# Three waits tied by hand around the merge of two attention branches

## The chip, the core and the metric

The kernel runs on one NeuronCore of a Trainium2 chip, in float32. The metric is the device time of one execution in microseconds. Its engines are TensorE (PE in the profile, with PEld for its weight loads), VectorE (DVE), ScalarE (ACT), GpSimd (POOL) and SyncE (SP, which here only issues DMAs). Each works through its own instructions in order and waits for others by semaphores. DMAs are issued from the queues of SP, ACT or POOL: an issue that waits holds up all that stands behind it in that queue.

## The reference

One layer on 512 tokens plus 16 learned meta tokens, width 1024. The normalised input `xn` goes into two attention branches of 8 heads each, `o_sb` (stick-breaking) and `o_df` (differential, with a norm of its own for each head). Cut to what the change touches:

```python
o_df = (rmsnorm(o_df, subln_g[l]) * (1.0 - lam_init)).transpose(0, 2, 1, 3).reshape(B, L_pad, DF_V_W)
y_sb = o_sb @ w_br_sb[l]
y_df = o_df @ w_br_df[l]
gates = jax.nn.sigmoid(xn @ w_gate[l] + b_gate[l]).reshape(B, L_pad, 2, D)
merged = gates[:, :, 0] * y_sb + gates[:, :, 1] * y_df
h = h + merged @ w_out[l]
```

Then follow a SwiGLU feed-forward part with a residual and a last norm.

## The kernel before

**Products.** Every float32 operand is held as a high part (rounded to the matmul's format) and a low part, the rest. `split` (lines 77 to 79) makes them: ScalarE casts the high part (`wh`, L78), VectorE subtracts to get the low one (`wl`, L79). A product is three matmuls per 128 rows of the contraction: L290 (high by high), L291 (high weight by low activation) and L292 (low weight by high activation). PE can so start on a weight when `wh` is there, and stops at the first L292 when `wl` is not.

**Weights.** They come in chunks of 512 KB in a fixed list (`stream`), loaded by SP into three `wst` buffers and split two chunks ahead of use. A buffer is loaded again when its `wl` is done.

**The gates.** `gate` (L805) computes one block of 128 channels (f, of 8) of one branch's gate (br, 0 or 1) for all 512 tokens: 24 matmuls into one PSUM bank, of which there are four for this, then an evacuation by ScalarE with the bias (L807). The gates of f = 0 are computed early and stored in DRAM (`g_part`). Those of f = 1 and 2 (`sg0`, `sg1`) are computed during the last two heads; their evacuation adds the bias, and their sigmoids are taken in place at L1053. From f = 3 on the evacuation itself is a sigmoid.

**The last head's norm.** `norm` in `df_head` (L767 to L776) takes a Ln and an Exp on ScalarE (L771, L772), two products on VectorE (L773, L774), and makes the head's output `o_h` on ScalarE (L775) and `o_l` on VectorE (L776). The last head's norm is run between the matmuls of the gates of f = 2.

**The branch outputs.** `y_units` multiplies two heads at a time with a slice of the branch's weight (matmuls named `o_h`, `o_l`), evacuates each f on ScalarE (L796, into `y_out`) and stores it from GpSimd's queue into DRAM with an accumulating DMA (L800, `y_df<-y_out`).

**The merge** (from L1055). For f in the order 1, 2, 0, 3 to 7: SP loads the sums back (`y_sb`, `y_df`, L1065), two f ahead. They lie in memory that the attention used before, so the first of these loads wait for the attention's last reader. GpSimd multiplies gate and output in place (L1122; VectorE for f = 6 and 7), VectorE adds the two products (L1126, into `mf` for f below 4), and `merge_sums` (L1087) splits the sum and combines it with others for the output product, which is made of seven products of half size. Each branch has two gate tiles, so f = 0 uses the tiles of f = 1 again: the stored gates are loaded into them (L1117) once the sum of f = 1 is done, and only then comes their sigmoid (L1118). The residual `x` is loaded into `hres` from GpSimd's queue, four DMAs of 512 KB (L1133).

**What sets the order.** Past the start, a scheduler puts each engine's instructions in order by its own estimate of when they can run; the order is then fixed. `tc.add_manual_dep` tells it that one instruction comes behind another. Activation table loads are put in where a function is not in the set that is loaded.

## Time and profile before

| | |
|---|---|
| median of 3 runs | 950.56 us (948.53 to 2375.36) |
| profiled execution, its own time | 949.31 us |
| its span, first to last instruction | 947.5 us |
| instructions in the span | 16049 |
| mean granted clock of TensorE | 0.997 |
| DMA moved | 158.41 MB, mean 167 GB/s |

Of the three runs two lie within 2 us of the profiled one. In the profile's rows a line such as `L79` is a line of the kernel; times in a timeline are microseconds from the start of the span, first the start, then the duration; what stands in brackets is how long the engine sat idle before and what ended that. A row of waits gives the total in us, the number of times and the longest.

### The profile page before, as it was taken

The page shows a single profiled execution, that of the slowest core. Times are in us where ns is not written, and L with a number is a line of the kernel's source. Part 1 is how long each engine was busy: PE and PEld are TensorE (multiplying, and loading weights), DVE is VectorE, ACT ScalarE, POOL GpSimd, SP SyncE. Part 2 cuts the span into 40 slices and gives each one's busy share as a digit, 9 for nine tenths or more (in the row PEclk, how much of TensorE's full clock was granted, in tenths as well). Part 3 has the DMA queues.
Part 4 walks back from the last instruction along what each step waited for, and adds up shares of the span by engine and source line. Part 5 has one row for each costly group of instructions (what it writes and reads, how often), then busy time and mean ns, then how long its engine had stood idle before and what let it go on. Part 6 is the DMA issues. An engine that isn't in the chain of part 4 may idle for free.

```text
span 947.5 us, 16049 instructions
## 1 busy us (share of the span) xinstructions
PE 929.5 (98%) x6009; PEld 843.6 (89%) x6010; DVE 733.9 (77%) x1400; ACT 586.3 (62%) x1105; POOL 186.8 (20%) x211
## 2 busy tenths in 40 slices
PE   8999999999999999999999899999999999999997
PEld 5988999898999999999887688899999999978886
DVE  6988878776678766787653578899888888989875
ACT  6665676676656666666774355765555555566654
POOL 3000121222323344344504330001000000000013
PEclk9999999999999999999999999999999999999999
DMA  8525778778767889799958854537743343286642
GB/s 248 143 68 157 176 170 203 168 164 251 192 198 184 196 190 190 162 208 191 198 155 203 262 172 163 144 80 175 158 124 112 93 131 90 68 259 202 198 153 89
DMA packets 155823, 158.41 MB, mean 167 GB/s; under 512 B 6465, under 2 KB 117218, under 8 KB 155746
## 3 DMA queue, kind: packets, MB, share of 16 engines
q1 hardware_dynamic: 132690, 101.61, 35.9%
q0 software_dynamic: 22896, 55.72, 28.8%
q8 instruction: 47, 0.77, 0.3%
q14 instruction: 30, 0.25, 0.1%
q10 hardware_dynamic: 160, 0.07, 0.0%
HBM read 133.64 MB, written 50.86 MB: 195 GB/s over the span
## 4 chain that ended last, share of the span: by engine, by line
PE 76%; DVE 12%; issue 4%; ACT 3%; DMA 3%; POOL 1%; SPq 0%; POOLq 0%; ACTq 0%; DVEq 0%
PE mm L292 17%; PE mm L291 17%; PE mm L290 17%; PE z L290 6%; PE z L291 6%; PE z L292 6%; DVE wl L79 3%; DVE s L636 2%; PE z L705 1%; PE z L704 1%; ACT wh L78 1%; PE tr L555 1%; DMA wsu<-in_w_in_dram 1%; DVE s L637 1%; DVE s L632 1%
## 5 line engine op out<-in xcount | busy, mean ns | idle before, releaser
L292 PE MATMUL mm<-xT_h,wl 128*128 128x264 f32 (+2 forms) x656 | 213.5, 325 | 3.3 <-DVE wl L79 3.3
L291 PE MATMUL mm<-xT_l,wh 128*128 128x264 f32 (+2 forms) x656 | 214.3, 327 | 0.5
L290 PE MATMUL mm<-xT_h,wh 128*128 128x264 f32 (+2 forms) x656 | 214.3, 327 | 0.5 <-ACT xT_h L909 0.5
L79 DVE TENSOR_TENSOR wl<-wst,wh 128x1024 fp32r<-128x1024 f32 (+1 forms) x147 | 166.4, 1136 | 31.1 <-ACT wh L78 30.7
L78 ACT CAST wh<-wst 128x1024 fp32r<-128x1024 f32 (+1 forms) x147 | 141.8, 966 | 76.2 <-PE mm L291 55.2
L292 PEld LDWEIGHTS mm<-xT_h,wl 128*128 128x128 f32 x656 | 124.0, 189 | 13.7 <-DVE wl L79 3.7
L290 PEld LDWEIGHTS mm<-xT_h,wh 128*128 128x128 f32 x656 | 124.0, 189 | 10.4 <-ACT xT_h L909 0.9
L291 PEld LDWEIGHTS mm<-xT_l,wh 128*128 128x128 f32 x656 | 123.8, 189 | 10.4 <-DVE xT_l L910 1.3
L290 PE MATMUL mm<-hT_h,wh 128*128 128x256 f32 x304 | 85.9, 284 | 1.2 <-ACT qx L1317 0.8
L292 PE MATMUL mm<-hT_h,wl 128*128 128x256 f32 x304 | 85.9, 284 | 0.0
L291 PE MATMUL mm<-hT_l,wh 128*128 128x256 f32 x304 | 85.8, 283 | 0.0
L290 PEld LDWEIGHTS mm<-hT_h,wh 128*128 128x128 f32 x304 | 57.9, 191 | 1.8 <-ACT qx L1317 1.2
L292 PEld LDWEIGHTS mm<-hT_h,wl 128*128 128x128 f32 x304 | 58.1, 191 | 0.0
L291 PEld LDWEIGHTS mm<-hT_l,wh 128*128 128x128 f32 x304 | 58.1, 191 | 0.0
L708 DVE CUSTOM_DVE_ANT_0 pr<-z,bias 128x144 f32<-128x144 f32 (+3 forms) x64 | 30.9, 501 | 34.2 <-PE z L705 31.9
L290 PE MATMUL mm<-o_h,wh 128*128 128x512 f32 x128 | 53.2, 415 | 0.1
L291 PE MATMUL z<-wl,da 128*128 128x512 f32 (+1 forms) x132 | 50.4, 382 | 0.6 <-DVE wl L79 0.6
L291 PE MATMUL mm<-o_l,wh 128*128 128x512 f32 x128 | 50.1, 391 | 0.3 <-DVE o_l L776 0.3
L290 PE MATMUL z<-wh,da 128*128 128x512 f32 (+1 forms) x132 | 50.3, 381 | 0.0
L1432 POOL TENSOR_TENSOR outs<-hres,gF 128x512 f32<-128x512 f32 x4 | 6.2, 1548 | 223.6 <-DVE hres L1418 216.8
L292 PE MATMUL z<-wh,da 128*128 128x512 f32 (+1 forms) x132 | 50.2, 380 | 0.0
L292 PE MATMUL mm<-o_h,wl 128*128 128x512 f32 x128 | 50.2, 392 | 0.0
(366 smaller groups left out, 2515.5 us busy)
## 6 DMA issues: line engine op xcount, KB each, us to landing
wst<-in_w_in_dram SPq DMA_DIRECT2D x40, 512.0 KB, 5.9
ds<-in_w_ffn_down_dram POOLq DMA_DIRECT2D x30, 512.0 KB, 6.1
wst<-in_w_ffn_gate_dram SPq DMA_DIRECT2D x22, 512.0 KB, 4.0
wsu<-in_w_ffn_up_dram SPq DMA_DIRECT2D x20, 512.0 KB, 3.8
wst<-in_w_gate_dram SPq DMA_DIRECT2D x16, 512.0 KB, 8.6
y_df<-y_out POOLq DMA_DIRECT2D x32, 256.0 KB, 7.2
slots<-ds SPq DMA_DIRECT2D x13, 512.0 KB, 3.3
os<-in_w_out_dram POOLq DMA_DIRECT2D x12, 512.0 KB, 4.6
```

The costliest lines, as they stand in the source:

```text
L78: cast["last"] = (hi_copy or nc.scalar.copy)(hi, src)
L79: (lo_eng or nc.vector).tensor_tensor(lo, src, hi.bitcast(F32), op=ALU.subtract)
L290: nc.tensor.matmul(ps, lhsT=ah, rhs=bh, start=(start and i == 0), stop=False, skip_group_check=skip)
L291: nc.tensor.matmul(ps, lhsT=ah, rhs=bl, start=False, stop=False, skip_group_check=skip)
L292: nc.tensor.matmul(ps, lhsT=al, rhs=bh, start=False, stop=(stop and i == n - 1), skip_group_check=skip)
L555: nc.tensor.transpose(pt[:, (t - j) * P:(t - j + 1) * P], blocks(t, j * P, (j + 1) * P), ident)
L632: nc.vector.scalar_tensor_tensor(s, zz, 0.0, e, op0=ALU.max, op1=ALU.add)
L636: nc.vector.tensor_tensor_scan(f, resets[:, L - (b - a):][:, ::-1], f, BIG, op0=ALU.mult, op1=ALU.add)
L637: nc.vector.tensor_tensor(s, zz, s, op=ALU.subtract)
L704: nc.tensor.matmul(o, lhsT=q[c][:, qs], rhs=k[c][:, 0, k0:k1], start=True, stop=False)
L705: nc.tensor.matmul(o, lhsT=q[c][:, qs], rhs=k[c][:, 1, k0:k1], start=False, stop=True)
L708: nc.vector.tensor_tensor_reduce(po, zz, bb, scale=1.0, scalar=-3.0e38, op0=ALU.add, op1=ALU.max, accum_out=mx[:, t, c:c + 1])
```

## The change

Three ties are added with a new helper, `behind(ins, name)`, which makes an instruction wait for one that was remembered in `cast` under that name.

```diff
     def split(hi, lo, src, lo_eng=None, hi_copy=None):
         cast["last"] = (hi_copy or nc.scalar.copy)(hi, src)
-        (lo_eng or nc.vector).tensor_tensor(lo, src, hi.bitcast(F32), op=ALU.subtract)
+        cast["lo"] = (lo_eng or nc.vector).tensor_tensor(lo, src, hi.bitcast(F32), op=ALU.subtract)
+
+    def behind(ins, name):
+        tc.add_manual_dep(ins.ins, cast[name].ins.name,
+                          mybir.DependencyInfo(mybir.DependencyClass.Sync, mybir.DependencyReason.DATA))
...
         split(wh, wl, staged[n], nc.gpsimd if n < 3 else None)
+        cast["split"] = cast["lo"]
...
-            nc.scalar.activation(sq, sq, AF.Exp, scale=-0.5)
+            cast["norm"] = nc.scalar.activation(sq, sq, AF.Exp, scale=-0.5)
...
     for sg in sg0 + sg1:
-        nc.scalar.activation(sg, sg, AF.Sigmoid)
+        behind(nc.scalar.activation(sg, sg, AF.Sigmoid), "norm")
...
-            (nc.gpsimd if f < 6 else nc.vector).tensor_tensor(sg[br], sg[br], y, op=ALU.mult)
+            if f < 6:
+                cast["gated"] = nc.gpsimd.tensor_tensor(sg[br], sg[br], y, op=ALU.mult)
+            else:
+                nc.vector.tensor_tensor(sg[br], sg[br], y, op=ALU.mult)
...
-        nc.vector.tensor_tensor(m, sg[0], sg[1], op=ALU.add)
+        merged = nc.vector.tensor_tensor(m, sg[0], sg[1], op=ALU.add)
+        if 2 < f < KT - 1:
+            behind(merged, "split")
...
     for t in range(NQ):
-        nc.gpsimd.dma_start(hres[:, t], xv[:, t])
+        behind(nc.gpsimd.dma_start(hres[:, t], xv[:, t]), "gated")
```

The sum of two gated outputs (f = 3 to 6) comes behind the last weight's low part that the program has asked for, the loads of `hres` behind GpSimd's last product, and the four sigmoids of f = 1 and 2 behind the last norm's Exp. (The helper also replaces the two lines in `c2` that did the same by hand.) No operation is added to what the kernel computes. Lines behind the edits have larger numbers in the new kernel: L771 becomes L775, L775 L779, L800 L804, L1053 L1057, L1122 L1127, L1133 L1142. The scheduler, given the ties, moves a few instructions.

ScalarE's queue around the last head's norm, before. `sq` is the norm's variance, `sg_...` a gate tile, `wh` a weight's high part, `o_h` the head's output:

```order
L78 CAST sqh_5819<-sq_5818 128x512
L771 ACT_TABLE_LOAD
L771 ACTIVATE sq_5818<-tr_5846,eps_c_179 128x512
L807 ACTIVATE sg_5825<-mm_5827,pcol_165 128x512
L772 ACT_TABLE_LOAD
L772 ACTIVATE sq_5818<-sq_5818 128x512
L78 CAST wh_5944<-wst_5828 128x1024
L1053 ACT_TABLE_LOAD
L1053 ACTIVATE sg_5825<-sg_5825 128x512
L775 ACTIVATE o_h_5216<-of_5817,g_sub_177 128x512
```

The same place in the new kernel:

```order
L78 CAST sqh_5819<-sq_5818 128x512
L775 ACTIVATE sq_5818<-tr_5846,eps_c_179 128x512
L776 ACTIVATE sq_5818<-sq_5818 128x512
L1057 ACT_TABLE_LOAD
L1057 ACTIVATE sg_5577<-sg_5577 128x512
L811 ACTIVATE sg_5825<-mm_5827,pcol_165 128x512
L779 ACTIVATE o_h_5216<-of_5817,g_sub_177 128x512
L78 CAST wh_5944<-wst_5828 128x1024
L1057 ACTIVATE sg_5578<-sg_5578 128x512
L1057 ACTIVATE sg_5825<-sg_5825 128x512
```

Before, two of the four sigmoids and a table load stood ahead of the first row. Now all four come behind the Exp, and three of the four table loads are gone; a weight's cast has moved behind `o_h`. On VectorE the low part of that weight has likewise moved behind `o_l`, and that is the only move there.

GpSimd's queue at the start of the merge, before. The DMA rows are the accumulating stores of `y_df` (the number behind the name is f); `sg_5577` and `sg_5578` are the gates of f = 1, `sg_5825` that of f = 2:

```order
L800 DMA y_df_7_129<-y_out_3055 128x512
L800 DMA y_df_0_122<-y_out_3055 128x512
L1122 TENSOR_TENSOR sg_5577<-sg_5577,y_sb_6004 128x512
L800 DMA y_df_1_123<-y_out_3055 128x512
L1122 TENSOR_TENSOR sg_5825<-sg_5825,y_sb_6008 128x512
L800 DMA y_df_2_124<-y_out_3055 128x512
L800 DMA y_df_3_125<-y_out_3055 128x512
L800 DMA y_df_4_126<-y_out_3055 128x512
L1122 TENSOR_TENSOR sg_5578<-sg_5578,y_df_6006 128x512
```

In the new kernel:

```order
L804 DMA y_df_7_129<-y_out_3055 128x512
L1127 TENSOR_TENSOR sg_5577<-sg_5577,y_sb_6004 128x512
L1127 TENSOR_TENSOR sg_5825<-sg_5825,y_sb_6008 128x512
L804 DMA y_df_0_122<-y_out_3055 128x512
L804 DMA y_df_1_123<-y_out_3055 128x512
L804 DMA y_df_2_124<-y_out_3055 128x512
L804 DMA y_df_3_125<-y_out_3055 128x512
L804 DMA y_df_4_126<-y_out_3055 128x512
L1127 TENSOR_TENSOR sg_5578<-sg_5578,y_df_6006 128x512
```

The two products with `y_sb` have moved ahead of the stores of f = 0 and 1. On SP the loads of `y_sb` for f = 1 and 2 likewise moved ahead of one load of a gate's weight.

GpSimd's queue a little later, before; `sg_6036` and `sg_6037` are the gates of f = 0, `sg_6054` and `sg_6055` those of f = 3:

```order
L1122 TENSOR_TENSOR sg_6036<-sg_6036,y_sb_6012 128x512
L1133 DMA hres_6463<-in_x_dram 128x1024
L1122 TENSOR_TENSOR sg_6037<-sg_6037,y_df_6014 128x512
L1133 DMA hres_6463<-in_x_dram 128x1024
L1122 TENSOR_TENSOR sg_6054<-sg_6054,y_sb_6024 128x512
L1133 DMA hres_6463<-in_x_dram 128x1024 x2
L1122 TENSOR_TENSOR sg_6055<-sg_6055,y_df_6026 128x512
```

In the new kernel, where the last four products are those of f = 4 and 5:

```order
L1127 TENSOR_TENSOR sg_6036<-sg_6036,y_sb_6012 128x512
L1127 TENSOR_TENSOR sg_6037<-sg_6037,y_df_6014 128x512
L1127 TENSOR_TENSOR sg_6054<-sg_6054,y_sb_6024 128x512
L1127 TENSOR_TENSOR sg_6055<-sg_6055,y_df_6026 128x512
L1127 TENSOR_TENSOR sg_6132<-sg_6132,y_sb_6038 128x512
L1127 TENSOR_TENSOR sg_6133<-sg_6133,y_df_6040 128x512
L1127 TENSOR_TENSOR sg_6216<-sg_6216,y_sb_6056 128x512
L1127 TENSOR_TENSOR sg_6217<-sg_6217,y_df_6058 128x512
L1142 DMA hres_6463<-in_x_dram 128x1024 x4
```

The four loads of `hres` have moved from between the products of f = 0 and 3 to behind the last product. PE's order is the same in both kernels.

More of the change, by code (lines that the diff above doesn't have):

```diff
@@ L234, in c2 @@
         if f in (2, 3):
-            behind = mybir.DependencyInfo(mybir.DependencyClass.Sync, mybir.DependencyReason.DATA)
-            tc.add_manual_dep(first.ins, cast["hn" if f == 2 else "bf"].ins.name, behind)
+            behind(first, "hn" if f == 2 else "bf")
         nc.vector.tensor_tensor(s[:, K1], s[:, K2], g[:, K1], op=ALU.add)
```

## The prediction

> **What bounds the kernel now.** The page comes first.
>
> ```profile
> span 947.5 us, 16049 instructions
> PE 929.5 (98%) x6009; PEld 843.6 (89%) x6010; DVE 733.9 (77%) x1400; ACT 586.3 (62%) x1105; POOL 186.8 (20%) x211
> ```
>
> TensorE (PE) is busy for 929.5 of 947.5 us. The change adds and removes no matmul, so it can win only what lies in the other 18 us, and what a slow clock costs. The next view is that of the waits, for the matmuls alone.
>
> ```profile
> PE mm L292 <- DVE wl L79: 3.3, 1, 3.3
> ...
> PE mm L290 <- ACT qx L1317: 0.8, 1, 0.8
> ...
> PE mm L291 <- DVE o_l L776: 0.3, 1, 0.3
> ```
>
> The longest wait of the kernel happens once: a matmul of L292 waits 3.3 us for the low part `wl` of a weight. The last line is a wait for `o_l`, the last attention head's output; the one between is in the feed-forward part, and no wait past 540 us is longer than it. The first and the last lie in the stretch that the change touches, as the busy time in windows of 10 us shows (columns: window, length, PE, PEld, DVE, ACT, POOL, granted clock, share of the DMA engines, GB/s).
>
> ```profile
> 490.00:500.00 10.00, 9.68 (x41) 7.11 (x39) 3.73 (x5) 8.78 (x10) 0.00 (x0) 1.00 0.02 7
> 500.00:510.00 10.00, 9.90 (x43) 8.19 (x44) 4.20 (x3) 6.37 (x11) 6.59 (x7) 1.00 1.00 233
> ...
> 520.00:530.00 10.00, 10.00 (x46) 8.29 (x45) 4.33 (x8) 2.72 (x7) 2.85 (x4) 1.00 0.95 229
> 530.00:540.00 10.00, 6.70 (x22) 4.80 (x21) 6.92 (x7) 4.49 (x7) 6.49 (x8) 0.83 0.80 277
> ```
>
> From 530 to 540 only 22 matmuls are started instead of some 45, and the mean clock is 0.83. PE's timeline prices both places.
>
> ```profile
> 498.83 0.39 PE L292 MATMUL mm<-o_h,wl 128*128 128x512 f32 x1
> ...
> 500.44 0.40 PE L292 MATMUL mm<-o_h,wl 128*128 128x512 f32 x1
> ...
> 531.54 0.39 PE L291 MATMUL mm<-xT_l,wh 128*128 128x512 f32 x1
> 531.77 0.39 PE L292 MATMUL mm<-xT_h,wl 128*128 128x512 f32 x1
> ...
> 532.54 0.40 PE L291 MATMUL mm<-xT_l,wh 128*128 128x512 f32 x1
> 536.19 0.80 PE L292 MATMUL mm<-xT_h,wl 128*128 128x512 f32 x1 [3.25 <-DVE wl L79]
> ...
> 539.34 0.39 PE L290 MATMUL mm<-xT_h,wh 128*128 128x512 f32 x1
> ```
>
> The steady step is 531.77 - 531.54 = 0.23 us. Four losses follow. (a) From 498.83 to 500.44 are three steps, 1.61 us instead of 0.68: 0.93 lost on `o_h` and `o_l`. (b) From 531.77 to 532.54 are two steps, 0.77 instead of 0.46: 0.31 lost, at the start of the gate of f = 5, whose PSUM bank ScalarE frees. (c) From 532.54 to 536.19 is one step, 3.65: 3.42 lost on `wl`. (d) From 536.19 to 539.34 are seven steps, 3.15 instead of 1.60: 1.55 lost, because the clock is halved after the stall. Together 6.2 us. That is the most that the change can win here, 0.7%.
>
> **Part 1: the sigmoids behind the last norm.** ScalarE's and VectorE's rows around that norm:
>
> ```profile
> 490.53 1.28 ACT L771 ACT_TABLE_LOAD   x1 [0.80 <-DVE sql L79]
> 491.82 0.69 ACT L771 ACTIVATE sq<-tr,eps_c 128x512 f32<-128x512 f32 x1
> 493.13 0.69 ACT L807 ACTIVATE sg<-mm,pcol 128x512 f32<-128x512 f32 x1 [0.62 <-PE mm L292]
> 493.84 1.28 ACT L772 ACT_TABLE_LOAD   x1
> 495.13 0.63 ACT L772 ACTIVATE sq<-sq 128x512 f32<-128x512 f32 x1
> ...
> 496.73 1.28 ACT L1053 ACT_TABLE_LOAD   x1
> 498.02 0.63 ACT L1053 ACTIVATE sg<-sg 128x512 f32<-128x512 f32 x1
> 498.56 0.71 ACT L775 ACTIVATE o_h<-of,g_sub 128x512 fp32r<-128x512 f32 x1
> ```
>
> ```profile
> 489.76 0.69 DVE L79 TENSOR_TENSOR sql<-sq,sqh 128x512 fp32r<-128x512 f32 x1 [0.69 <-ACT sqh L78]
> 495.80 0.75 DVE L773 SCALAR_TENSOR_TENSOR sq<-tr,var_max,sq 128x512 f32<-128x512 f32 x1 [5.35 <-ACT sq L772]
> 496.59 0.69 DVE L774 TENSOR_TENSOR of<-of,sq 128x512 f32<-128x512 f32 x1
> ...
> 499.30 0.75 DVE L776 SCALAR_TENSOR_TENSOR o_l<-of,g_sub,o_h 128x512 fp32r<-128x512 f32 x1 [0.89 <-ACT o_h L775]
> ```
>
> The Ln and the Exp each have a table load of 1.28 us before them, since sigmoids ran earlier; the Exp also stands behind an evacuation (L807) that waits for PE. In the new order the Ln needs no load: `sql` is done at 490.45, its two matmuls of 0.39 end about 491.2, and the Ln starts there. The Exp follows at once: 491.2 + 0.69 + 0.63 = 492.5. VectorE's two steps end at 492.5 + 0.75 + 0.69 = 494.0. Meanwhile ScalarE loads the sigmoid's table, runs one sigmoid and the evacuation: 492.5 + 1.28 + 0.63 + 0.69 = 495.1. Then `o_h` is done at 495.8 and `o_l` at 496.5, where before it was 500.05. PE wants `o_h` at 499.06, so loss (a), 0.93 us, goes, and 2.5 us of cover remain. Three table loads are gone; that in itself is worth nothing more.
>
> **Part 2: what `o_l` releases.** The loads of the branch outputs `y_sb` take memory of the attention, and wait for that `o_l`.
>
> ```profile
> 500.18 0.81 SPq L1065 DMA_DIRECT2D y_sb<-y_sb  x2
> ```
> ```profile
> 504.27 1.28 POOL L1122 TENSOR_TENSOR sg<-sg,y_sb 128x512 f32<-128x512 f32 x1 [1.65 <-DMA y_sb<-y_sb]
> 505.52 0.85 POOL L800 DMA_DIRECT2D y_df<-y_out  x1
> ```
> ```profile
> DMA to landing us min/median/max: 2.7/4.3/6.0
> ```
>
> In the new order they can start at 496.6, into DMA engines that are idle (share 0.02 from 490 to 500). The last row is the landing time of the eight `y_sb` loads; I take 3.5, between the least and the median, as the engines are idle: 500.1. GpSimd's queue now has both `y_sb` products ahead of the accumulating stores of `y_df`: 500.1 + 2 x 1.28 = 502.7, then the store of f = 0 (0.85), and the store of f = 1 starts at 503.5 instead of 505.52. That is 2.0 us earlier; with landings of 2.7 and 4.3 it is 2.8 and 1.2. From here hangs the chain that ends in loss (c): that store, the load of `y_df`, the product of f = 1, the merge sum that frees its gate tile, the load of the stored gate of f = 0 into it, its sigmoid, its products, its merge sum, and behind this on VectorE the `wl` for which PE waits. I carry the 2.0 through unchanged.
>
> **Part 3: the residual's loads behind GpSimd's products.**
>
> ```profile
> 530.73 0.60 POOL L1133 DMA_DIRECT2D hres<-in_x_dram  x1
> 531.34 1.31 POOL L1122 TENSOR_TENSOR sg<-sg,y_df 128x512 f32<-128x512 f32 x1
> ...
> 533.17 1.27 POOL L1122 TENSOR_TENSOR sg<-sg,y_sb 128x512 f32<-128x512 f32 x1
> ```
> ```profile
> 531.47 0.67 ACT L807 ACTIVATE sg<-mm,pcol 128x512 f32<-128x512 f32 x1
> ```
> ```profile
> 532.68 2.32 DVE L1126 TENSOR_TENSOR mf<-sg 128x512 f32<-128x512 f32 x1 [1.62 <-POOL sg L1122]
> 534.92 1.21 DVE L79 TENSOR_TENSOR wl<-wst,wh 128x1024 fp32r<-128x1024 f32 x1
> ```
>
> Two issues of `hres` go from between the products of f = 0 and f = 3. On the old clock the second product would start at 530.73 and end at 532.04; the third starts when its gate is evacuated (531.47 + 0.67 = 532.14) instead of at 533.17. VectorE's sum of f = 0 takes 2.32 us here where others take 0.69: it ends 0.48 after GpSimd's third product (534.44, then `wl` at 534.92). I take that as blocking, which comes again: the sum ends 1.0 us earlier. The loads themselves move to about 556 and are wanted much later:
>
> ```profile
> 573.70 0.68 DVE L1207 TENSOR_TENSOR hres<-hres,mm 128x512 f32<-128x512 f32 x1
> ```
> ```profile
> DMA to landing us min/median/max: 4.0/5.0/6.5
> ```
>
> Four issues of 0.6 and a landing of 6.5 (second row, the four `hres` loads) end near 565: some 8 us of cover, cost nothing.
>
> **Part 4: the merge sums tied behind the weight splits.** VectorE's order from the first merge sum on is the same in both kernels, and both instructions are on one engine, so nothing waits that did not: 0. The sum of f = 0, before which PE stalls, is not among the tied ones (3 to 6).
>
> **The sum.** PE comes to the gate of f = 5 without (a): its L290 is due at 531.77 + 0.23 - 0.93 = 531.07, its first L292 at 531.53. Its bank is free at 532.14 - 2.0 = 530.14, so loss (b) goes. The wait for `wl` ends at 536.19 - 2.0 - 1.0 = 533.2: a loss of 1.67 stays of (c). For (d) the trace has one case, a gap of 3.25 us that halved the clock, and (a), two short gaps that did not. A gap of 1.7 is nearer to the latter, so I take (d) as gone. The gain is 6.21 - 1.67 = 4.5 us. The Trainium skill, "TensorE: Matmul & The Clock Gate", Part 1 (The HAM clock gate), has the clock judged in free-running windows of 3.4 us, of which one idle window halves it; by that 1.7 us could not fill one, and the trace agrees so far that the half clock lasted 3.4 us.
>
> The profiled execution took 949.31 us, the median of the three runs is 950.56 and the lowest 948.53. So 949.31 - 4.5 = 944.8, and as a median, which scatters by a microsecond, **945**. Past 540 PE waits for others 0.8 us at most at a time and the other engines' orders stay, so a shift reaches the end. PE then runs 4.5 us earlier and the chain behind the gates 3.0: the gates after f = 5 lose 1.5 us of what cover they have.
>
> **The rivals.**
> - *The half clock stays* although the stall is shorter: the gain is 4.5 - 1.55 = 3.0, 946.3. For it: nothing shows how short a gap must be. 13%.
> - *VectorE gets ahead of GpSimd* at the sum of f = 0: then it takes 0.69 from 530.1, `wl` is done at 532.0, the loss is 0.5: gain 5.7, 943.6. Against it: at 532.68 VectorE began before GpSimd's 533.17 and was still the one held up, 2.32 against 1.27. 12%. The Trainium skill, "SBUF — State Buffer", section "SBUF: two separate sides", says that whichever of the two starts first keeps the shared port for its whole instruction; that would be this rival, and the row disagrees.
> - *The transfers are the bound, not the order*: with DMA shares of 1.00 and 0.95 between 500 and 530 the gate of f = 0 lands when it did. Then only Part 3's 1.0 is won at `wl` (535.2), PE, due at 531.53, loses 3.67 and the half clock stays: 6.21 - 5.22 = 1.0, 948.3. Against it: the first loads start 3.5 us earlier into idle engines. 14%.
> - *GpSimd's queue is held up by its two new front places*, slower than before: if `o_l` comes no earlier in practice, `y_sb` lands at 504.27 again, both products run first (506.8), and the store of f = 1 starts at 507.7, 2.2 late. Less 1.0 of Part 3, `wl` and all behind it are 1.2 later: 950.5. It decides at 504.7, which is 505.52 less one issue: if the second product ends later, the chain loses. Against it: no row stands in the way of `o_l`. 8%.
> - The forecast, 944.8 with 944.0 to 945.6 for the landings of 2.7 and 4.3, has the other 53%.
>
> **Range and chances.** From 943.0, below the second rival by the scatter, to 949.6, which takes in the third: it leaves out the slower rival and little else. All cases lie within 2% (931.5 to 969.7), about what a measurement of this kernel can tell from no change: 0.98, with 0.01 on either side.
>
> **What would show it.** Right: one table load, not four, between 478 and 500; `o_l` near 496.5; no PE wait for `o_l`; `y_sb` loads near 496.6 and the store of f = 1 near 503.5; PE's wait for `wl` under 2 us and the clock at 1.00 from 530 to 540. Wrong: the wait still over 3 us, a window with half clock, a second `y_sb` product that ends after 504.7, or a new PE wait between 540 and 620, for weights that `hres` delays or for `hres` itself.

## The result, and the profile after

| | before | after |
|---|---|---|
| median | 950.18 us | 943.99 us (942.70 to 944.09) |
| ratio, 95% interval | | 0.9937 [0.9918, 0.9957] |
| profiled execution | 949.31 us | 942.70 us |
| its span | 947.5 us | 940.9 us |

The changed kernel is 0.6% faster, less than the 2% that counts as a difference; the interval leaves out 1. One of the four executions of before took 2375.36 us; the ratio leaves it out, and the median of the other three is 949.81. Line numbers past the diff's first hunk are 4 to 9 higher now: L290 to L292 are L294 to L296, the norm's L771 to L776 are L775 to L780, L807 is L811, L1053 is L1057, L1065 is L1069, L1117 and L1118 are L1121 and L1122, L1122 is L1127, L1126 is L1133, L1133 is L1142; in the experiments they differ by a few again.

The page's head, and of the waits the matmuls' own:

```profile
span 940.9 us, 16049 instructions
...
PE 925.6 (98%) x6010; PEld 842.0 (89%) x6010; DVE 731.7 (78%) x1400; ACT 582.3 (62%) x1102; POOL 188.2 (20%) x211
```
```profile
PE mm L294 <- ACT qx L1326: 0.8, 1, 0.8
...
PE mm L296 <- DVE wl L79: 0.5, 1, 0.5
```

The wait of 3.3 us for `wl` is 0.5, the one for `o_l` is gone, and ScalarE has three instructions fewer (1102 for 1105), the table loads. The same windows as before (window, length, PE, PEld, DVE, ACT, POOL, granted clock, share of the DMA engines, GB/s):

```profile
490.00:500.00 10.00, 9.93 (x44) 8.22 (x45) 4.46 (x6) 8.53 (x13) 0.97 (x1) 1.00 0.26 72
...
530.00:540.00 10.00, 9.51 (x43) 7.50 (x42) 6.29 (x10) 4.04 (x7) 2.26 (x2) 1.00 0.61 168
```

From 530 to 540 PE starts 43 matmuls instead of 22, at the full clock; the half clock is gone. PE's timeline at the two places:

```profile
498.37 0.39 PE L296 MATMUL mm<-o_h,wl 128*128 128x512 f32 x1
...
530.78 0.39 PE L295 MATMUL mm<-xT_l,wh 128*128 128x512 f32 x1
531.66 0.50 PE L296 MATMUL mm<-xT_h,wl 128*128 128x512 f32 x1 [0.49 <-DVE wl L79]
...
533.40 0.40 PE L294 MATMUL mm<-xT_h,wh 128*128 128x512 f32 x1
```

The first and the last of these are the matmuls that stood at 498.83 and 539.34 before. The **stretch** between them has 151 steps and took 40.51 us; now it takes 533.40 - 498.37 = 35.03. At the steady step it would be 34.3 (40.51 less the prediction's 6.2 of losses). So 5.5 us were won here, and 0.7 is still lost. The remaining 1.1 of the profiles' 6.6 us lie elsewhere: 0.46 of it ahead of the first of these matmuls (498.83 against 498.37), the rest behind the last. In the profiles below the first matmul's start alone scatters by more (497.95 to 500.40). The stretch, which doesn't depend on these parts, is the measure used from here on.

What ScalarE, VectorE, SP and GpSimd did on the way there, from the last norm to the second store:

```profile
490.84 0.69 ACT L775 ACTIVATE sq<-tr,eps_c 128x512 f32<-128x512 f32 x1 [1.55 <-PE tr L774]
491.56 0.63 ACT L776 ACTIVATE sq<-sq 128x512 f32<-128x512 f32 x1
492.20 1.28 ACT L1057 ACT_TABLE_LOAD   x1
```
```profile
495.35 0.75 DVE L780 SCALAR_TENSOR_TENSOR o_l<-of,g_sub,o_h 128x512 fp32r<-128x512 f32 x1 [1.65 <-ACT o_h L779]
```
```profile
496.23 0.82 SPq L1069 DMA_DIRECT2D y_sb<-y_sb  x2
...
519.21 0.86 SPq L1121 DMA_DIRECT2D sg<-g  x2
```
```profile
499.03 3.57 POOL L1127 TENSOR_TENSOR sg<-sg,y_sb 128x512 f32<-128x512 f32 x2 [23.85 <-DMA y_sb<-y_sb]
502.55 4.41 POOL L804 DMA_DIRECT2D y_df<-y_out  x5
```

One table load stands where four stood, `o_l` is done at 496.1, the `y_sb` loads go at 496.2, GpSimd's two products end at 502.6 and the stores follow. The stored gates of f = 0 are asked for at 519.21. Before, that was

```profile
521.05 1.78 SPq L1117 DMA_DIRECT2D sg<-g  x2
```

1.84 us later. Then VectorE's sum of f = 0, the weight split for which PE waits, and GpSimd's product beside them:

```profile
528.68 0.69 DVE L1133 TENSOR_TENSOR mf<-sg 128x512 f32<-128x512 f32 x1 [1.76 <-POOL sg L1127]
529.29 2.31 DVE L79 TENSOR_TENSOR wl<-wst,wh 128x1024 fp32r<-128x1024 f32 x1
```
```profile
528.87 1.65 POOL L1127 TENSOR_TENSOR sg<-sg,y_sb 128x512 f32<-128x512 f32 x1 [0.23 <-ACT sg L811]
```

The sum takes 0.69 instead of 2.32. The split behind it, 1.21 before, now takes 2.31: it ends 1.1 us after GpSimd's product (530.52). The hold has moved by one instruction. The residual's loads moved to 553.77 and landed in 5.7 to 8.1 us (before: 4.0 to 6.5), by 564.1 at the latest; they are first used at 569.17, and nothing waited for them.

### The profile page after: what moved, and what is told of

It reads as the page before. It is cut to its first block, busy times and chain, and to the rows that moved or that the text cites. A ratio compares the mean times of both kernels' runs of the same rounds, so it can differ in the third digit from the quotient of the medians.

```text
span 940.9 us, 16049 instructions
## 1 busy us (share of the span) xinstructions
PE 925.6 (98%) x6010; PEld 842.0 (89%) x6010; DVE 731.7 (78%) x1400; ACT 582.3 (62%) x1102; POOL 188.2 (20%) x211
## 4 chain that ended last, share of the span: by engine, by line
PE 79%; DVE 11%; issue 3%; ACT 3%; DMA 1%; POOL 1%; SPq 0%; ACTq 0%; POOLq 0%; DVEq 0%
PE mm L295 18%; PE mm L296 18%; PE mm L294 18%; PE z L294 6%; PE z L296 6%; PE z L295 6%; DVE wl L79 3%; DVE s L640 2%; PE z L709 1%; PE z L708 1%; PE tr L559 1%; DVE s L641 1%; DVE s L636 1%; PE tr L535 1%; POOL y_df L804 1%
## 5 line engine op out<-in xcount | busy, mean ns | idle before, releaser
L294 PE MATMUL mm<-xT_h,wh 128*128 128x264 f32 (+2 forms) x656 | 213.6, 326 | 0.5 <-ACT xT_h L913 0.5
L296 PE MATMUL mm<-xT_h,wl 128*128 128x264 f32 (+2 forms) x656 | 212.7, 324 | 0.5 <-DVE wl L79 0.5
L296 PEld LDWEIGHTS mm<-xT_h,wl 128*128 128x128 f32 x656 | 123.5, 188 | 10.9 <-DVE wl L79 0.9
L294 PEld LDWEIGHTS mm<-xT_h,wh 128*128 128x128 f32 x656 | 123.4, 188 | 9.9 <-ACT xT_h L913 0.9
L294 PE MATMUL mm<-hT_h,wh 128*128 128x256 f32 x304 | 85.8, 284 | 1.4 <-ACT qx L1326 0.8
L296 PE MATMUL mm<-hT_h,wl 128*128 128x256 f32 x304 | 85.9, 283 | 0.0
L294 PEld LDWEIGHTS mm<-hT_h,wh 128*128 128x128 f32 x304 | 57.9, 191 | 2.0 <-ACT qx L1326 1.3
L296 PEld LDWEIGHTS mm<-hT_h,wl 128*128 128x128 f32 x304 | 58.0, 191 | 0.0
L294 PE MATMUL mm<-o_h,wh 128*128 128x512 f32 x128 | 53.0, 414 | 0.0
L294 PE MATMUL z<-wh,da 128*128 128x512 f32 (+1 forms) x132 | 50.2, 381 | 0.0
L296 PE MATMUL z<-wh,da 128*128 128x512 f32 (+1 forms) x132 | 50.2, 380 | 0.0
L296 PE MATMUL mm<-o_h,wl 128*128 128x512 f32 x128 | 50.1, 391 | 0.0
## 6 DMA issues: line engine op xcount, KB each, us to landing
wst<-in_w_in_dram SPq DMA_DIRECT2D x40, 512.0 KB, 6.1
ds<-in_w_ffn_down_dram POOLq DMA_DIRECT2D x30, 512.0 KB, 6.0
wst<-in_w_ffn_gate_dram SPq DMA_DIRECT2D x22, 512.0 KB, 3.9
wsu<-in_w_ffn_up_dram SPq DMA_DIRECT2D x20, 512.0 KB, 4.0
wst<-in_w_gate_dram SPq DMA_DIRECT2D x16, 512.0 KB, 6.4
slots<-ds SPq DMA_DIRECT2D x13, 512.0 KB, 3.3
os<-in_w_out_dram POOLq DMA_DIRECT2D x12, 512.0 KB, 4.6
```

The costliest lines, as they stand in the source:

```text
L294: nc.tensor.matmul(ps, lhsT=ah, rhs=bh, start=(start and i == 0), stop=False, skip_group_check=skip)
L296: nc.tensor.matmul(ps, lhsT=al, rhs=bh, start=False, stop=(stop and i == n - 1), skip_group_check=skip)
```

## The experiments

Where an edit below isn't spelled out, `behind` is the change's helper. e3, e4 and e7 make a weight split, or half of it, a second time with the same result; all others compute what the kernel computes. The medians of before stood at 948.2 to 949.9 us beside these runs.

### One part at a time: e1, e2, e9

e1 has the change without the tie of the residual's loads, e2 without the tie of the sigmoids. Both leave out the ties of the merge's sums, which move no instruction on any engine.

```diff
# e1
-        behind(nc.gpsimd.dma_start(hres[:, t], xv[:, t]), "gated")
+        nc.gpsimd.dma_start(hres[:, t], xv[:, t])
# e2
-        behind(nc.scalar.activation(sg, sg, AF.Sigmoid), "norm")
+        nc.scalar.activation(sg, sg, AF.Sigmoid)
```

> Only the sigmoids are tied behind the last norm; the merge sums and the residual's loads are free again, so that only the four residual loads stand between GpSimd's products once more. Theory (the early o_l carries most of the gain, the residual's loads about 1 us): no PE wait for o_l, stores of y_df as early as in the changed kernel, the sum of f = 0 ends about 1.0 us later than there, PE waits about 1.5 to 1.7 us for wl, the clock stays whole; time about 1.0 us above the changed kernel's 944.0, so 945.0. Rival (the residual's loads carry the gain at wl): the wait is back at 3 us with the half clock, 948 or more.

Measured: 946.85 us, ratio 0.9988 [0.9972, 1.0004], 1.9 us above the 945.0 that was expected. Beside the changed kernel's later 945.15 and 943.72 (e5 and e10 below, with before at 948.2 in all three) it is 1.7 and 3.1 us more, where the theory had 1.0.

> Only the residual's loads are tied behind GpSimd's products. Theory: the loss at o_l (0.93 us) stays, the chain up to the stored gates of f = 0 lands as before, wl comes 1.0 us earlier (near 535.1), PE still waits 2.2 to 2.7 us. Gain over before 1.0 us if the half clock stays (949.2), 2.5 if it goes (947.7). Rival (the residual's loads carry the gain): wait under 1 us, 945 or less.

Measured: 945.88 us, ratio 0.9978 [0.9965, 0.9992]. The expectation counted from a before of 950.2 us; beside its own, 948.25, e2 gains 2.4 us, what the theory has if the half clock goes (2.5). PE's wait speaks against the theory all the same: it is 0.2 us, not 2.2 to 2.7. By its median e2 gains 1.0 us more than e1, though their intervals overlap; of the 2.5 us between their stretches (38.27 in e1, 35.73 in e2) some 1.5 are e1's half clock. So the part that the prediction priced at 1.0 us, the residual's loads, seems to give more alone than the part priced at 2.0 plus loss (a). e1's waits, its stretch of half clock, and GpSimd and VectorE before it:

```profile
PE mm L296 <- DVE wl L79: 2.3, 1, 2.3
```
```profile
533.50:534.00 0.50, 0.32 (x1) 0.32 (x2) 0.47 (x3) 0.00 (x0) 0.00 (x0) 0.50 1.25 291
```
```profile
526.19 1.29 POOL L1127 TENSOR_TENSOR sg<-sg,y_sb 128x512 f32<-128x512 f32 x1 [5.83 <-ACT sg L1122]
528.22 0.60 POOL L1140 DMA_DIRECT2D hres<-in_x_dram  x1 [0.75 <-DMA y_df<-y_out]
528.83 1.32 POOL L1127 TENSOR_TENSOR sg<-sg,y_df 128x512 f32<-128x512 f32 x1
530.05 0.58 POOL L1140 DMA_DIRECT2D hres<-in_x_dram  x1
530.64 1.29 POOL L1127 TENSOR_TENSOR sg<-sg,y_sb 128x512 f32<-128x512 f32 x1
```
```profile
530.18 2.31 DVE L1133 TENSOR_TENSOR mf<-sg 128x512 f32<-128x512 f32 x1 [2.42 <-POOL sg L1127]
```

The stored gates are asked for at 519.08 in e1, 1.97 us earlier than before, about the 2.0 forecast of the sigmoids' tie, though not by the path forecast (Part 2 below). But the first load of the residual waits in GpSimd's queue for a store to land (until 528.22) and takes 0.6 itself, with the second product of f = 0 behind it; and the sum that this product releases is held for 2.31 us, until after the next product. The wait and the hold are the price of the loads' place, and the prediction had seen only the issues and the hold.

e2 has no issue there. Its sum and split:

```profile
529.95 0.69 DVE L1133 TENSOR_TENSOR mf<-sg 128x512 f32<-128x512 f32 x1 [1.41 <-POOL sg L1127]
530.56 2.32 DVE L79 TENSOR_TENSOR wl<-wst,wh 128x1024 fp32r<-128x1024 f32 x1
```

It keeps loss (a), and its stored gates are asked for at 520.57, only 0.5 earlier than before, yet its stretch is only 0.7 us longer than the changed kernel's. Not all of that is the loads' place: in this execution ScalarE had the first stored gate 5.7 us after it was asked for (526.26 - 520.57), in before's profile 7.7, and that wait ends ahead of the residual's loads. What the loads themselves cost is worked out below, under Part 3.

e9 has the ties of the sums and nothing else.

```diff
+        if 2 < f < KT - 1:
+            behind(merged, "split")
```

> The kernel before with only the ties of the merge's sums, which the prediction put at nothing since every engine's instructions keep their order. Theory: ratio 1.000 within its interval. Its profile is also a second look at the same order as before: if the 7.7 and 8.4 us that the two loads of stored gates took in the first one are that execution's own, they land in 5.5 to 7 us here, the sum of f=0 starts some 10.5 us behind their issue instead of 11.6, and TensorE's wait at the merge is 1.5 to 3.3 us. Rival: the ties cost something (waits on semaphores in VectorE's queue), 1 us or more, or the long landing comes back because of the order: 7.5 to 8.5 us again.

Measured: 947.76 us, ratio 0.9995 [0.998, 1.0011]. The ties cost and give nothing. Since the order is that of before, its profile is a second sight of it:

```profile
PE mm L296 <- DVE wl L79: 2.2, 1, 2.2
```
```profile
530.00:540.00 10.00, 7.83 (x35) 6.13 (x34) 6.21 (x7) 3.67 (x6) 6.11 (x7) 1.00 0.97 305
```
```profile
531.57 2.33 DVE L1133 TENSOR_TENSOR mf<-sg 128x512 f32<-128x512 f32 x1 [2.27 <-POOL sg L1127]
```

The wait is 2.2 us and the clock stays whole: the stretch takes 37.67 us, 2.8 less than in the profile on which the prediction was costed, with every instruction in the same place. The sum starts 531.57 - 521.02 = 10.6 us after the stored gates are asked for, not 11.6. Part of the 6.2 us of losses was that one execution's.

### How long a wait halves the clock: e3, e4, e7

The changed kernel with VectorE's split of gate (0, 5), the one PE waits for, made once more in full (e3), one and a half times more (e4), or half a time more (e7).

```diff
# in generic(n), e3; e4 adds a second line with wl[:, 0:4] and so on; e7 has only that second line
+        if stream[n][0] == ("gate", 0, 5):
+            nc.vector.tensor_tensor(wl, staged[n], wh.bitcast(F32), op=ALU.subtract)
```

> The changed kernel, with the low part of the weight of gate (0, f = 5) made twice, the same values again; the second time stands behind one more split, so PE's gap before its first L292 of that gate grows from 0.5 to about 2.0 us. Theory (a gap well under 3 us leaves the clock whole): 1.5 us slower than the changed kernel, 945.5, clock 1.00 throughout. Rival (a gap of 2 us halves the clock): another 1.5 us, 947.0, and a window at 0.50.

Measured: 946.73 us, ratio 0.9991 [0.9977, 1.0004], between the theory's 945.5 and the rival's 947.0. Both seem to happen: of its ten executions the five with a mean granted clock of 0.998 or more have a median of 945.98 us, the five below it 947.60. The profiled one, with the half clock, is the slowest (949.43).

> As the run with the gap of 2 us, and half of the low part a third time: a gap of about 3.1 us, nearly the 3.25 of the kernel before. Theory (the half clock came from the length of the gap): the clock is halved for 3.4 us behind it, 2.6 + 1.5 us slower than the changed kernel, 948.1. Rival (it depends on where the gap falls in time, or needs more than 3.1 us): no half clock, 946.6.

Measured: 949.22 us, ratio 1.0013 [0.9999, 1.0028]; the theory had 948.1, counted from 944.0. It is 4.1 us above e5, the theory's 2.6 + 1.5.

> The changed kernel with half of the weight split of gate (0, 5) made a second time (0.68 us of VectorE more in front of TensorE's next matmul, and with the small split ahead of it about 1.1). It lengthens TensorE's wait at the merge from 0.5 to about 1.6 us, near the 1.67 us that the prediction forecast for the change. Theory: a wait of that length leaves the granted clock whole, as the prediction had it: time up by 1.1 us against e5. Rival: the clock halves for a stretch of 3.4 us as with the waits of 2.3, 2.4 and 3.1 us seen so far: up by 2.8.

Measured: 945.57 us, ratio 0.9973 [0.9952, 0.9995], 0.4 above e5 (theory 1.1, rival 2.8). Of each profile the row of waits and the windows around the half clock, e3 first, then e4, then e7, whose wait has the same row as e3's:

```profile
PE mm L298 <- DVE wl L225: 2.4, 1, 2.4
```
```profile
535.00:540.00 5.00, 4.44 (x12) 3.50 (x13) 2.83 (x5) 1.94 (x3) 1.74 (x1) 0.66 0.38 108
```
```profile
PE mm L299 <- DVE wl L226: 3.1, 1, 3.1
```
```profile
531.71:535.12 3.41, 1.39 (x7) 0.81 (x5) 3.41 (x3) 0.26 (x1) 0.96 (x1) 1.00 0.53 154
535.12:538.53 3.41, 2.31 (x6) 1.83 (x7) 2.61 (x5) 1.94 (x3) 0.92 (x1) 0.50 0.20 54
538.53:541.95 3.42, 3.42 (x10) 2.65 (x9) 1.60 (x4) 0.90 (x3) 0.81 (x1) 0.50 0.69 204
541.95:545.36 3.41, 3.41 (x16) 2.81 (x15) 2.59 (x3) 2.98 (x4) 1.88 (x2) 1.00 0.44 129
```
```profile
530.00:540.00 10.00, 7.61 (x27) 5.84 (x26) 7.32 (x10) 2.75 (x5) 2.90 (x2) 0.83 0.50 151
```

e7 was meant to wait 1.6 us; its wait became 2.4, since VectorE's sum of f = 0 was held for 1.77 us in that execution, as in e5 below, and not 0.69. So it tells nothing about 1.6 us, but it adds a point: waits of 2.32 (e1), 2.36 (e3) and 2.39 us (e7) halved the clock for about 3.4 us, the wait of 3.12 (e4) for 6.8. Waits of 1.57, 1.77, 1.95 and 2.17 us (e5, e12, e6, e9) left it whole. By length alone the border lies between 2.2 and 2.3 us in these profiles. But e4's clock halves at 535.12, when its wait (533.10 to 536.22) has lasted 2.02 us, less than e9's 2.17: length is not what decides. The last section says what does.

### The changed kernel again: e5, e10

> The changed kernel once more, unaltered, on the chip of the four runs above, where the kernel before had a median of 948.25 us. On its own chip the change gave a ratio of 0.9937, which would be 942.3 us here. Theory: the two parts help one another at one place (each of them alone leaves a wait of TensorE there), so the whole gives more than the sum of the two alone (946.85 and 945.88, that is 1.4 and 2.4 us off, together 3.8): 942.3 to 943.5, no half clock at 530 to 540 in the profile, the wait for the split of the weights under 1 us. Rival: the parts only add, 944.5, and the first comparison's gain of 6.2 was in part a matter of the chip.

Measured: 945.15 us, ratio 0.9973 [0.9957, 0.999], above the theory's 942.3 to 943.5 and nearer to the rival's 944.5. It ran on another chip than e1 to e4, but before took as long there (948.23 and 948.25 us).

> The changed kernel a third time. The first comparison gave a ratio of 0.9937, the second 0.9973. Theory: the two differ by where the loads of stored gates land in each execution (TensorE's wait at the merge was 0.5 us in one profile and 1.6 in the other), so the ratio lies between: 0.995 to 0.997. Rival: the chip decides, and the ratio is again at one of the two ends, as the median of before is 950 (0.9937) or 948 (0.9973).

Measured: 943.72 us, ratio 0.9945 [0.9927, 0.9962], between the two earlier ratios and just below the theory's range. The gains of e1 and e2, 1.4 and 2.4 us, together 3.8, lie between the 3.1 of e5 and the 4.5 of e10: that the parts help one another is not shown. Of e5 the sum and GpSimd's product beside it:

```profile
530.05 1.77 DVE L1133 TENSOR_TENSOR mf<-sg 128x512 f32<-128x512 f32 x1 [1.19 <-POOL sg L1127]
```
```profile
529.99 1.29 POOL L1127 TENSOR_TENSOR sg<-sg,y_sb 128x512 f32<-128x512 f32 x1
```

Same program, another execution: both stored gates landed close together, so GpSimd ran its products back to back, the third began 0.06 us ahead of VectorE's sum instead of 0.19 behind it, and the sum was held (1.77 us). PE's wait is 1.6 us, the stretch 36.11. In e10 the products run back to back too, but the sum is 0.05 us ahead of the third: it takes 0.69 again, the wait is 0.4 and the stretch 34.90. So the program's order leaves open which of the two engines comes first, and a few hundredths of a microsecond decide it each time. That accounts for some 1 us between executions; it doesn't account for all of the difference between the three comparisons (gains of 6.2, or 5.8 without the execution of 2375.36 us, then 3.1 and 4.5 us). The last two were made on different chips; what the rest of the difference is stays open.

### Who stands behind whom: e6, e8, e11, e12

e6 puts one of the four loads of the residual back, behind the second product of f = 0 (remembered as "mid").

```diff
+                if (f, br) == (0, 1):
+                    cast["mid"] = cast["gated"]
...
-        behind(nc.gpsimd.dma_start(hres[:, t], xv[:, t]), "gated")
+        behind(nc.gpsimd.dma_start(hres[:, t], xv[:, t]), "gated" if t else "mid")
```

> The changed kernel with one of the four loads of the residual put back between GpSimd's products, behind the second product of f=0 (the one that releases VectorE's sum of f=0); the other three stay behind the last product. Both profiles that have a load issued there show that sum at 2.3 us, the four that have none at 0.69 us. Theory: the issue puts the next product ahead of the sum, so the sum takes 2.3 us, the split of the weights behind it 1.2 unhindered, and it ends 1.1 us (0.6 of it the issue's own time in GpSimd's queue, if the store that it waits for has landed) later than in the changed kernel: TensorE's wait 1.6 instead of 0.5, time up by 1.1 us against e5, or by 2.8 if that wait also halves the clock for a stretch. Rival: whoever comes first goes first, with or without an issue in between: the sum stays at 0.69 us, the split begins before the next product and takes 1.2 instead of 2.3, and TensorE's wait is gone: time down by 0.5.

Measured: 945.13 us, ratio 0.9974 [0.9955, 0.9993], no different from e5 in time. VectorE, then GpSimd:

```profile
530.25 0.69 DVE L1135 TENSOR_TENSOR mf<-sg 128x512 f32<-128x512 f32 x1 [1.97 <-POOL sg L1127]
530.86 2.65 DVE L79 TENSOR_TENSOR wl<-wst,wh 128x1024 fp32r<-128x1024 f32 x1
```
```profile
530.52 0.60 POOL L1144 DMA_DIRECT2D hres<-in_x_dram  x1 [0.30 <-POOL sg L1127]
531.12 1.29 POOL L1127 TENSOR_TENSOR sg<-sg,y_sb 128x512 f32<-128x512 f32 x1
```

Neither account holds. The sum took 0.69 us, against the theory. The split began 0.26 us before the product, and by the rival it should have gone first; it took 2.65 and ended 1.1 us after the product. So here, too, the VectorE instruction that starts while GpSimd issues a load, with a product right behind, is held by that product. PE's wait was 1.95 us.

e8 and e11 are one kernel: the changed one, with GpSimd's product of f = 3 (first branch) tied behind the split for which PE waits.

```diff
+                if (f, br) == (3, 0):
+                    cast["held"] = cast["gated"]
...
# in generic(n)
+        if stream[n][0] == ("gate", 0, 5):
+            behind(cast["held"], "lo")
```

> The changed kernel with one tie more: GpSimd's product of f=3 by the first branch waits for the weight split that TensorE waits for at the merge. Theory: the split (2.3 us in the changed kernel, beside a product of GpSimd) takes 1.2 us, TensorE's last 0.5 us of wait there is gone with the slow start behind it, 0.7 us off against e5, and the product, 1.7 us later, has its successors' time to spare. Rival: the product's delay comes back as a later sum of f=3 and a wait further on, or the split is held by a transfer instead: no change or up by 0.5.

Measured: 943.93 us, ratio 0.9954 [0.9937, 0.9971], beside e5's 945.15.

> The kernel of e8 (GpSimd's product of f=3 behind the weight split) once more, beside the changed kernel. Theory: faster than it by 0.7 to 1.3 us, with a narrower spread, since in no execution the product can take VectorE's port from the split, and the wait at the merge stays under the length that halves the clock. Rival: its 1.2 us in the first comparison were scatter: no difference.

Measured: 942.72 us, ratio 0.9938 [0.992, 0.9955], beside e10's 943.72. In e8:

```profile
530.10 0.69 DVE L1137 TENSOR_TENSOR mf<-sg 128x512 f32<-128x512 f32 x1 [1.98 <-POOL sg L1129]
530.71 1.22 DVE L79 TENSOR_TENSOR wl<-wst,wh 128x1024 fp32r<-128x1024 f32 x1
```
```profile
532.06 1.36 POOL L1129 TENSOR_TENSOR sg<-sg,y_sb 128x512 f32<-128x512 f32 x1 [1.99 <-ACT mg_h L78]
```

Both VectorE instructions run unheld, and no matmul waits for `wl` at this place any more. The stretch takes 34.57 us in e8 and 34.23 in e11, the steady step's 34.3. The gain on the changed kernel is 1.2 and 1.0 us, about what that kernel still lost (0.6 to 1.8 us in its three profiles). The narrower spread that was expected shows in the first pair (2.7 us against e5's 6.2), not in the second (3.2 against e10's 2.1). It is the fastest of these kernels by its medians, though the intervals of the two overlap in each comparison.

e12 has this tie alone, on the kernel before.

> The kernel before (with the ties of the merge's sums, which measured nothing) and, of all else, only the tie of e8: GpSimd's product of f=3 behind the weight split. The sigmoids and the residual's four loads stay where they were (one of the loads moves ahead of that product). Theory: what the change's place is worth is in large part the time that VectorE stands behind this one product, so the sum takes 0.7 us instead of 2.3 and the split 1.2, TensorE's wait there falls from 2.2 to 3.3 us to 0.6 to 1.7 with the clock whole: a ratio of 0.997 to 0.998, about what the loads' move alone gave. Rival: the loads' issues in GpSimd's queue and their transfers hold the sum back all the same: 1.000.

Measured: 946.38 us, ratio 0.9981 [0.996, 1.0002]. The stretch takes 37.21 us, 0.5 less than e9's; the sum takes 0.69 us, the wait is 1.8, just above the 0.6 to 1.7 expected, and the clock whole. The tie removes the hold, but the sum still starts 531.58 - 520.62 = 11.0 us after the stored gates are asked for: the residual's load in the queue keeps that. The ratio is what the theory expected; its interval doesn't exclude the rival's 1.000.

### The place in numbers

From each profile: when the stored gates are asked for, from there to the start of the sum of f = 0, the sum's duration, from the sum's start to the end of the split for which PE waits, PE's wait, the stretch. The kernels of e3, e4 and e7 have a longer split by design and are left out.

| | asked for | to the sum | sum | to the split's end | wait | stretch |
|---|---|---|---|---|---|---|
| before | 521.05 | 11.6 | 2.32 | 3.5 | 3.3 | 40.51 |
| e9, order of before | 521.02 | 10.6 | 2.33 | 3.5 | 2.2 | 37.67 |
| e12, e9 with the product held | 520.62 | 11.0 | 0.69 | 1.8 | 1.8 | 37.21 |
| e1, without the loads' tie | 519.08 | 11.1 | 2.31 | 3.4 | 2.3 | 38.27 |
| e2, without the sigmoids' tie | 520.57 | 9.4 | 0.69 | 2.9 | 0.2 | 35.73 |
| after | 519.21 | 9.5 | 0.69 | 2.9 | 0.5 | 35.03 |
| e5, after | 519.70 | 10.4 | 1.77 | 2.9 | 1.6 | 36.11 |
| e10, after | 519.79 | 9.3 | 0.69 | 2.9 | 0.4 | 34.90 |
| e6, one load back | 519.82 | 10.4 | 0.69 | 3.3 | 2.0 | 36.47 |
| e8, product held | 520.08 | 10.0 | 0.69 | 1.8 | 0.0 | 34.57 |
| e11, product held | 520.03 | 9.4 | 0.69 | 1.8 | 0.0 | 34.23 |

## Why the prediction was right

The time, 945.0 against 943.99, and its case came true: PE waits under 2 us for `wl`, with the clock whole. The mechanism is the one forecast, an earlier `wl`, but one of its steps failed (Part 2), two sizes were off, and chance helped the number. The forecast gain was 4.5 us; the three comparisons measured 6.2, 3.1 and 4.5. By its own steps:

- **The losses of before** (6.2 us) were right for the profile they were read from. As a measure of the order they were too high: the same order lost 3.4 in e9 (37.67 - 34.3). The half clock (d) was not a property of that order; in e9 the wait left the clock whole, and from e9's profile the same sum would have given 3.4 - 1.67 = 1.7 us and not 4.5. That the 1.55 us of (d) stood in the profile was luck. A single profile gives no sign of this; the scatter of many executions does. Beside e8, the 16 executions of before with a mean granted clock of 0.998 or more have a median of 947.1 us, the nine with 0.996 or less one of 950.7; the twelve of e8, without the wait, are all at 0.998 or more, from 942.3 to 945.0 us.
- **Part 1** was right: one table load, `o_l` at 496.1 (forecast 496.5), loss (a) gone.
- **Part 2** was right as far as GpSimd's queue. The loads went at 496.2 (496.6); they landed in 2.8 us, not 3.5, but the two products took 3.6 us, not 2.6, two misses that cancel, and ended at 502.6 (502.7). Nothing held the queue up, the slower rival, decided at 504.7, didn't happen, and the store of f = 1 went at 503.1 (503.5), 2.4 us earlier than before. The next step, "I carry the 2.0 through unchanged", failed. SP's load of `y_df` for f = 1 waits for that store to land, and the store took 7.6 us, before 5.7. SP's longest wait for such a store and its loads, before, then after:

```profile
SPq L1065 <- DMA y_df<-y_out: 5.4, 2, 3.2
```
```profile
511.25 2.96 SPq L1065 DMA_DIRECT2D y_df<-y_df  x2
```
```profile
SPq L1069 <- DMA y_df<-y_out: 8.2, 2, 7.3
```
```profile
510.76 1.59 SPq L1069 DMA_DIRECT2D y_df<-y_df  x2
```

  The load went 0.5 us earlier, and over the profiles of the table not at all: it is asked for between 510.0 and 512.0 us with the sigmoids' tie and without. What arrived at the stored gates, 1.84 us in the first profile and 1.97 in e1, came mostly from the load's own landing: the product behind it began 4.58 us after it (515.34), before 5.95 (517.20). By the table the stored gates are asked for at 519.7 on average with the tie (seven profiles) and at 520.8 without it (before, e9, e12, e2): some 1.1 us, not 2.0. Why the store and the load take so different times in the two orders is not shown.
- **Part 3** was sized at 1.0 us, and the runs give about 1.2. With loads issued ahead of the product that releases the sum, the way to the sum is 10.6 to 11.6 us, on average (11.6 + 10.6 + 11.0 + 11.1) / 4 = 11.1; in the other seven profiles of the table it is 9.3 to 10.4, on average 9.8. That is 1.3, but 0.6 of it lies ahead of the loads: ScalarE began on the second stored gate 8.2 us after the issue on average in the four, and 7.6 in the seven. The other 0.7, and 0.5 to 0.6 from the sum to the split (3.5 and 2.9), are the loads'. The reading "the second product would start at 530.73" took out the issue's own 0.6 and not its wait for a store to land, which lasts 0.75 us in e1; in the profile of before the store had landed, so nothing showed it. And the blocking "which comes again" fell on the sum only in e5 (and in e7); where the sum went first, the split behind it was held instead.
- **Part 4** was right: nothing (e9, 0.9995).
- **The sum.** The term mis-sized was what stays of (c): 1.67 forecast, and 0.88 - 0.23 = 0.65 in the first profile (530.78 to 531.66 is one step). In e5 the same wait left 1.7, in e10 less than 0.6. The first profile beat the forecast since its stored gates landed early: the rows of the first sigmoid, 5.4 us after the issue, and of before, 7.7 after it:

```profile
524.63 0.63 ACT L1122 ACTIVATE sg<-sg 128x512 f32<-128x512 f32 x1 [3.88 <-DMA sg<-g]
```
```profile
528.77 0.63 ACT L1118 ACTIVATE sg<-sg 128x512 f32<-128x512 f32 x1 [6.19 <-DMA sg<-g]
```

  That is a difference between executions and not of the order: in e9 it is 527.01 - 521.02 = 6.0, in e5 526.58 - 519.70 = 6.9. It was luck: the split ended at 531.60, before at 536.13, so 4.5 us earlier where the forecast had 3.0, and 1.5 of the 4.5 is that the second stored gate was begun 7.4 us after the issue (526.64) and not 8.9 (529.99).
- **The clock.** That a wait of 1.7 us leaves it whole is confirmed by e5, e12 and e6 (1.57 to 1.95), with little room: in e4 2.02 us were enough to halve it.
- **The rivals.** The half clock that stays: not in the changed kernel's three profiles, though e5's wait of 1.57 us is only 0.45 short of the 2.02 that were enough in e4. VectorE ahead of GpSimd: it happened at the sum, in two of the three, and its price was wrong, because the product then holds the split: 0.5 us are won, not 1.2. The transfers as the bound: false in its time, since the stored gates were asked for 1.84 us earlier and landed earlier, but half right in its cause: a store that went 2.4 us earlier landed only 0.5 earlier (Part 2). That the two parts' shares were nearly the reverse of what was forecast (e1 and e2) didn't show in the total.

## What to carry to other kernels

A DMA issue in the queue of an engine that also computes costs not only its own 0.6 us but its wait as well (0.75 us in e1), and whatever the next instruction then collides with; put it behind the last instruction that somebody waits for. Where two engines meet with 0.1 us between them, the profile of one execution shows one of two outcomes; a tie that fixes who goes first (e8) removes the wait. An earlier issue is not an earlier landing: a gain that passes through a DMA can't be carried through unchanged, as the store of f = 1 shows. And before a stall is costed, look at it in a second execution: here the same order lost 6.2 us in one profile and 3.4 in the next.

## What the runs showed of the hardware

**The clock halves after waits shorter than its window, and where the wait falls decides.** In these profiles the granted clock changes only at moments that lie a whole number of times 3.413 us apart. In before it falls at 535.91, rises at 539.32 and falls again at the kernel's end, at 945.51: once and 120 times 3.413. In e4 it is half from 535.12 to 541.95 (twice) and falls at 944.72 (120 times from the first). Counted back from the fall at the end, these moments cut every profile into windows of 3.413 us, also where the clock stayed whole at the merge (in e9 the end's fall is at 943.11, so windows end at 533.51 and 536.92). Each of the nine waits of over 1.5 us at this place, and its parts in the windows:

| | wait | parts | clock |
|---|---|---|---|
| e5 | 1.57 | 1.57 | whole |
| e12 | 1.77 | 1.77 | whole |
| e6 | 1.95 | 1.41, 0.54 | whole |
| e9 | 2.17 | 0.60, 1.57 | whole |
| e1 | 2.32 | 2.12, 0.20 | half for one window |
| e7 | 2.39 | 2.23, 0.16 | half for one window |
| e3 | 2.36 | 2.36 | half for one window |
| e4 | 3.12 | 2.02, 1.10 | half for two windows |
| before | 3.25 | 2.97, 0.28 | half for one window |

At the whole clock, a window with 1.77 us of the wait or less left it whole; one with 2.02 or more was followed by half clock, from the window's end on. In e4 the second window, with 1.10 us of the wait, kept the clock half; with 0.28 or less it rose again. So e9's 2.17 us were harmless because a window ended within them, and in e3 the clock fell at 535.76, 0.2 us after the wait was over. By where it falls, such a wait costs nothing more or some 1.5 us, loss (d) of the prediction. The Trainium skill, "TensorE: Matmul & The Clock Gate", Part 1 (The HAM clock gate), has free-running windows of 3.4 us and throttles after one idle window. The windows agree; that a whole window must be idle does not: 2.02 us of 3.41 were enough.

**GpSimd's product holds VectorE's instruction, and not only when it starts first.** The Trainium skill, "SBUF — State Buffer", section "SBUF: two separate sides", gives the shared port to whoever starts first, for the whole instruction. Seven meetings agree: e5's sum, 0.06 us behind the product, was held; the sums of after, e2 and e10, ahead of it, were not, and the splits behind these three, 0.41 to 0.56 us after the product's start, were held (2.31 to 2.32 us). Four disagree: in before, e9 and e1 the sum, and in e6 the split, started 0.26 to 0.49 us before the product by the profile, and were held until it ended. In all four GpSimd was just issuing a load of the residual, with the product next in its queue. An issue alone doesn't do it: in e12 the sum starts 0.10 us into the issues of two such loads, with no product right behind them, and takes its 0.69 us (VectorE, then GpSimd):

```profile
531.58 0.69 DVE L1137 TENSOR_TENSOR mf<-sg 128x512 f32<-128x512 f32 x1 [2.41 <-POOL sg L1129]
```
```profile
531.48 1.11 POOL L1146 DMA_DIRECT2D hres<-in_x_dram  x2
```

Nor does an accumulating store's issue with a product behind it: in e5 the sum of f = 1 starts at 517.15 within such an issue (517.07, 0.87 us), with the product at 517.65, and takes 0.69 us; there the product is the longer one (1.60).

Whether a product can have the port earlier than its row says, or a load's issue differs from a store's, is not settled.

**Landing times of the same 256 KB load differ by 1.5 us and more between executions of one order.** ScalarE began on the first of the two stored gates 7.7 and 6.0 us after its issue in before and e9, and 5.4, 6.9 and 5.9 us after it in the changed kernel's three profiles.
